# Attention weights transposed by TensorE instead of by DMA, in rounds of three steps placed inside the gemm pieces

## The chip, the cores and the metric

The program runs on one core of a Trainium2 chip. The metric is the device time of one execution in microseconds. Before the change the median of three runs is 3235.93 us (3235.06 to 3238.74).

## The reference

One inference step of a decoder layer. A prompt of 2048 tokens and eight sample tokens go through the same weights, all in float32:

- Mixers: `z = rms_norm(x) @ w_in` with 2304 columns, cut into q, k, v of mixer A (8 heads of 64) and of mixer B (8 query heads, 2 key heads). Mixer A attends in three branches, which are banded attentions over every token, every 4th and every 16th (`DIL_GROUPS = ((128, 1), (512, 4), (2048, 16))`), merged per position by their softmax denominators. Mixer B is banded over 128 keys with a sink per head. Each band: scores of 128 queries against one or two blocks of 128 keys, softmax, weights times values.
- Output projection of both mixers, then cross-attention into 256 memory tokens (its keys and values are `rms_norm(mem) @ w_mem_kv`).
- A feed-forward with a causal convolution of width 3: `w_up` (1024 to 5632), gate, `w_down` (2816 to 1024). Final norm.

The outputs are the prompt's and the samples' rows and the updated key and value caches, so large caches are copied as well.

## The kernel before

**Arithmetic.** A float32 operand is split into a rounded half `hi` (ScalarE) and the rest `lo` (VectorE, or GpSimd), and each product is three matmuls: hi·hi, lo·hi, hi·lo. `hi_of` and `lo_of` (L108 to L120) record these operations for every caller, so most of the splits stand at L110 and L120.

**Stage one** computes the input projection, the attention of both mixers, and the memory keys and values. The projection runs over four groups of 512 tokens and nine blocks of 256 columns, 144 tiles of 128 tokens by 256 columns; `ORDER` names the sequence of groups and columns. `gemm_tile` is one such tile, 24 matmuls of 256 columns (8 depths, three matmuls each; L672 to L674) into one of two PSUM banks `a`. `evac_in` applies rotary with four VectorE operations (or scales on ScalarE) and writes q, k, v to scratch in DRAM. When the columns of a group are done, its attention jobs are queued: kinds `d1`, `d4`, `d16` for mixer A's branches and `b` for mixer B, 64 jobs in all.

A job has two halves of four heads, here called half-jobs, 128 in all. 84 of them have two key blocks and 44 have one. `job_load` (L452, L457) reads a job's rows back from DRAM, and `job_prep` transposes its queries and keys on TensorE (`t_split`, `t_copy`, L473 and L482, through the two PSUM banks `t`) and splits them. A half-job then passes three steps:

- `stage_a`: scores into the banks `se` and `so` (L548; one bank each), masked with a running maximum on VectorE (L556, L559), exponential on ScalarE into `sm` (L561).
- `stage_b`: `sm` to a float16 pair `p2` (L569 ScalarE, L570 VectorE), then one DMA transpose of the whole pair into `pT`, issued on SP's queue (L572).
- `stage_c`: 20 matmuls of 64 columns per key block, `pT` times the values in three bfloat16 parts (L585), copied to `ost` (L592) and stored.

`attn_step` runs one step per call, and three calls are a round: `stage_a` of a new half-job with its `job_prep`, `stage_b` of the one before, and `stage_c` of the one whose transpose was issued two rounds earlier (the queue `ready`). `filler(n)` makes n calls behind each projection tile (2, 3 or 4) and 4 behind each of the 16 tiles of the memory gemm (`mem_gemm`, L1618 to L1620, same size). What is left runs after `mem_pieces`, and the PSUM pool of stage one closes (`p1.close()`) before stage two opens its own.

**Stage two** takes the prompt in four chunks of 512 tokens through output projection, cross-attention and feed-forward: `gemm_b` (L862 to L864), 512 columns a matmul, with the samples' attention, the merges and the cache copies as side work.

**Order.** The program text gives each instruction a priority; the scheduler (`schedule_with_timeline_sim=True`) then fixes the order in which every engine issues, and may place a later instruction ahead of one whose inputs it expects late. On the chip each engine keeps that order. This holds before and after the change, on TensorE too.

Of the kernel before, what the change touches and what calls it, by code (L numbers as in the profile page):

```python
# [35 lines left out]
def tile_layer(ctx: ExitStack, tc: tile.TileContext, I, C, O):  # L36
# [32 lines left out]
    mm = nc.tensor.matmul  # L69
    act = nc.scalar.activation  # L70
# [206 lines left out]
    nc.tensor.transpose(pv[:, 0:120], vrow, ident[:120, :120])  # L277
# [6 lines left out]
    def xprep(key, nxt=None):  # L284
# [3 lines left out]
        def norm():  # L288
            ss = sbL.tile([128, 1], F32, tag="ss", name="ss", bufs=3)
            junk = at_start("sm", 2) if key in range(4) else sbL.tile([128, 1024], F32, tag="xr", name="junk")  # L290
            act(out=junk[:rows], in_=x[:rows], func=ACTF.Square, accum_out=ss[:rows])
            r = sbL.tile([128, 1], F32, tag="r", name="r", bufs=18)
            rms_r(r[:rows], ss[:rows], 1.0 / D, 1, rows)
            rows_r[key] = r

        if key == "s":
            norm()
            pt = bank("t", 2)
            for k in range(8):
                nc.tensor.transpose(pt[:, k * NS:(k + 1) * NS], x[:NS, k * 128:(k + 1) * 128], ident[:NS, :NS])  # L300
# [13 lines left out]
        if key in (1, 2, 3):  # L314
            xr = at_start(*(("p2", 2), ("p2", 2), ("pT", 3))[key - 1]).rearrange("p (k t) -> p k t", k=8)
        else:
            xr = sbL.tile([128, 8, 128], F32, tag="xr", name="xr")
        for hf in range(2):
            pt = bank("t", 2)
            for k in range(4):  # L320
                kk = hf * 4 + k
                nc.tensor.transpose(pt[:, k * 128:(k + 1) * 128], x[:, kk * 128:(kk + 1) * 128], ident)
            act(out=xr[:, hf * 4:hf * 4 + 4, :], in_=pt.rearrange("p (k t) -> p k t", k=4), func=ACTF.Copy)
# [145 lines left out]
    def t_split(ins, hi, lo):  # L469
        pt = bank("t", 2)  # L470
        n = len(ins)
        for i, a in enumerate(ins):
            nc.tensor.transpose(pt[:, i * 128:(i + 1) * 128], a, ident)  # L473
# [4 lines left out]
    def t_copy(ins, out, eng="a"):  # L478
        pt = bank("t", 2)
        n = len(ins)  # L480
        for i, a in enumerate(ins):
            nc.tensor.transpose(pt[:, i * 128:(i + 1) * 128], a, ident)  # L482
        hi_of(out, pt[:, 0:n * 128].rearrange("p (k t) -> p k t", k=n), eng)

    def job_prep(job):
        job.full = job.kind == "d16" or (job.kind == "d4" and job.t == 0)
        if job.kind == "b":
            job.qh = sbR.tile([128, 4, 128], F32R, tag="qh", name="qh", bufs=2)
            job.ql = sbR.tile([128, 4, 128], F32R, tag="ql", name="ql", bufs=2)
            t_split([job.q[:, 128 * j:128 * j + 128] for j in range(4)], job.qh, job.ql)  # L490
            rh, rl = ring("b")
            s = job.t % 2
            t_split([job.k], rh[:, s], rl[:, s])
            job.kh, job.kl = rh, rl
        else:
            if job.full:
                job.qh = sbR.tile([128, 4, 128], F32, tag="qh", name="qf", bufs=2)
                job.kh = sbR.tile([128, 2, 4, 128], F32, tag="kh", name="kf", bufs=1)
                t_copy([job.q[:, 128 * j:128 * j + 128] for j in range(4)], job.qh)
                t_copy([job.k[:, 128 * j:128 * j + 128] for j in range(4)], job.kh[:, 1], "v")  # L500
                job.slots, job.vs, job.mo = [1], [job.v3], None
                job.ost = sbR.tile([128, ST], F32, tag="ost", name="ost", bufs=5)
# [3 lines left out]
            t_split([job.q[:, 128 * j:128 * j + 128] for j in range(4)], job.qh, job.ql)  # L506
            if job.kind == "d1":
                rh, rl = ring("d1")
                s = job.t % 2
            else:  # L510
                rh = sbR.tile([128, 2, 4, 128], F32R, tag="kh", name="kh", bufs=1)
                rl = sbR.tile([128, 2, 4, 128], F32R, tag="kl", name="kl", bufs=1)
                s = 1
            t_split([job.k[:, 128 * j:128 * j + 128] for j in range(4)], rh[:, s], rl[:, s])
            job.kh, job.kl = rh, rl
            if job.kind == "d4" and job.t > 0:
                t_split([job.kp[:, 128 * j:128 * j + 128] for j in range(4)], rh[:, 0], rl[:, 0])
                vprev["d4"] = job.vp3

        v3 = job.v3  # L520
        first = job.kind == "d16" or job.t == 0
        if first:
            job.slots, job.vs, job.mo = [s], [v3], None
        else:
            pv3 = vprev[job.kind]
            if s == 1:
                job.slots, job.vs, job.mo = [0, 1], [pv3, v3], 0
            else:
                job.slots, job.vs, job.mo = [0, 1], [v3, pv3], 1
        if job.kind in ("d1", "b"):  # L530
            vprev[job.kind] = v3
        job.ost = sbR.tile([128, ST], F32, tag="ost", name="ost", bufs=5)

    def stage_a(job, i):
# [15 lines left out]
        sm = sbR.tile([128, 4, 256], F32, tag="sm", name="sm", bufs=2)  # L550
# [62 lines left out]
    quads = deque()  # L613
    loaded = deque()
    pipe = {"b": None}
    ready = deque([None] * 2)
# [3 lines left out]
    def attn_busy():  # L620
        return bool(jobs or loaded or quads or pipe["b"] or any(ready))

    def attn_step():
        if not attn_busy():
# [3 lines left out]
        if s == 0:  # L628
            while len(loaded) < 2 and jobs:
                jb = jobs.popleft()  # L630
                job_load(jb)
                loaded.append(jb)
            if len(quads) == 0 and loaded:
                jb = loaded.popleft()
                job_prep(jb)
                quads.extend([(jb, 0), (jb, 1)])
            pipe["a"] = None
            if quads:
                jb, i = quads.popleft()
                pipe["a"] = (jb, i, stage_a(jb, i))  # L640
                if len(quads) == 0 and loaded:
                    jb = loaded.popleft()
                    job_prep(jb)
                    quads.extend([(jb, 0), (jb, 1)])
        elif s == 1:
            nxt = None
            if pipe["b"]:
                jb, i, sm = pipe["b"]
                nxt = (jb, i, *stage_b(jb, i, sm))
            pipe["b"] = pipe["a"]  # L650
            pipe["n"] = nxt
        else:
            ready.append(pipe["n"])
            if len(ready) > 2:
                e = ready.popleft()
                if e:
                    stage_c(*e)
# [37 lines left out]
    def mem_prep(t):  # L695

        if t == 0:
            while any(jb.kind != "b" for jb in [*jobs, *loaded, *(q[0] for q in quads)]):
# [9 lines left out]
        for hf in range(2):  # L708
            pt = bank("t", 2)
            for k in range(4):  # L710
                kk = hf * 4 + k
                nc.tensor.transpose(pt[:, k * 128:(k + 1) * 128], x[:, kk * 128:(kk + 1) * 128], ident)
# [27 lines left out]
    for oi, (g, js) in enumerate(ORDER):  # L740
        for j in js:
# [4 lines left out]
            for t in range(4):  # L746
# [3 lines left out]
                p = gemm_tile(u, *xT[tt])  # L750
# [4 lines left out]
                filler(4 if j in COLS_B else 2 if oi < 3 else 3)  # L755
# [53 lines left out]
    for a in range(3):  # L809
        n = 128 if a < 2 else 96  # L810
        nc.tensor.transpose(pt[:, a * 128:a * 128 + n], srow[:n, a, :], ident[:n, :n])
# [193 lines left out]
    def sample_softmax(S, nsl, nh, scale, sink, fix):  # L1005
# [6 lines left out]
        for i in range(nb):  # L1012
            nc.tensor.transpose(pt[:w, i * 128:(i + 1) * 128], Sf[:, i * w:(i + 1) * w], ident)
# [165 lines left out]
    def xs_begin():  # L1179
        p = [bankA("t"), bankA("t")]  # L1180
        row = panel32("qxrow")
        for k in range(8):
            nc.tensor.transpose(p[k // 4][:NS, (k % 4) * 128:(k % 4) * 128 + 128], qxs[:, k, :], ident)
# [32 lines left out]
    def xs_fin():  # L1216
        turn_in()
        p = bankA("t")
        for k in range(8):
            nc.tensor.transpose(p[:, k * NS:(k + 1) * NS], osab[:, k * 128:(k + 1) * 128], ident[:NS, :NS])  # L1220
# [20 lines left out]
    def heads_T(c, oT):  # L1241
# [3 lines left out]
        def one(k):  # L1245
            def go():
                pt = bankA("t")
                for i in range(4):
                    nc.tensor.transpose(pt[:, i * 128:(i + 1) * 128],
# [4 lines left out]
                if s_in:  # L1254
                    ps_ = bankA("t")
                    nc.tensor.transpose(ps_[:, 0:NS], osab[:, k * 128:(k + 1) * 128], ident[:NS, :NS])
# [9 lines left out]
    def pre(c, oT, begin):  # L1266
# [108 lines left out]
        def transp(h):  # L1375
            pe = p_t.pop(h)
            pn = [panel("pT"), panel("pT")]
            for kt in range(2):
                pt = bankA("t")
                for t in range(4):  # L1380
                    nc.tensor.transpose(pt[:, t * 128:(t + 1) * 128], pe[t // 2][:, t % 2, kt * 128:kt * 128 + 128], ident)
# [172 lines left out]
    def fin_steps(c, fin):  # L1554
# [4 lines left out]
        def turn(i, hf, pt):  # L1559
            a, n = fin.nt[i]  # L1560
            for k in range(4):
                nc.tensor.transpose(pt[:n, k * 128:(k + 1) * 128], xres[c, 4 * hf + k][:, a:a + n], ident)
# [50 lines left out]
    def mem_gemm(u, h, l):  # L1613
        p = bankA("t")
        for kt in range(8):
            wh, wl = u[kt // 4]
            q = kt % 4
            mm(p[:, 0:256], h[:, kt, :], wh[:, q, :], start=(kt == 0), stop=False)  # L1618
# [4 lines left out]
    def evac_mem(j, t, p, r):  # L1623
# [5 lines left out]
        if j < 4:  # L1629
            dma(out=p_mk[tok, cols], in_=z)  # L1630
            pt = bankA("t")
            for dt in range(2):
                nc.tensor.transpose(pt[:, dt * 128:dt * 128 + 128], z[:, dt * 128:dt * 128 + 128], ident)
# [6 lines left out]
    def mem_pieces():  # L1640
        for j in range(8):
            u = (W.get(), W.get())
            W.ahead(1)
            for t in range(2):
                evac_mem(j, t, mem_gemm(u, *MEM[t][:2]), MEM[t][2])
                filler(4)
# [22 lines left out]
    def conv_out(i):  # L1669
        def go():  # L1670
            gst = small("gst")[:110, 0:128]
            pt = bankA("t")
            nc.tensor.transpose(pt[:110, 0:128], gsave.rearrange("p j f -> p (j f)")[:, i * 110:(i + 1) * 110], ident)
# [83 lines left out]
```

## Time and profile before

| what | value |
|---|---|
| median of 3 runs | 3235.93 us |
| the profiled execution's own time | 3230.24 us |
| its span | 3228.5 us |
| TensorE busy, share of the span | 3100.5 us, 96% |
| VectorE busy | 2147.1 us, 67% |
| ScalarE busy | 1417.1 us, 44% |
| GpSimd busy | 1013.7 us, 31% |
| mean granted clock of TensorE | 0.984 |

The span runs from the first to the last instruction; 1.7 us of the execution's time lie around it. Matmuls are pipelined and the profile models their ends, so the busy share of TensorE says little of how full it is; the distance from one start to the next says more. Stage two begins with the first matmul of L862, at 999 us.

### The profile page before, as it was taken

Reading aid. Unit: us, or ns where it says so; the run is one execution under the profiler, and the core shown is the slowest. Engines: PE = TensorE matmul, PEld = TensorE weight load, DVE = VectorE, ACT = ScalarE, POOL = GpSimd, SP = SyncE. Lnnn points to the kernel's source line nnn. Section 1 sums busy time; section 2 is a strip of 40 time slices with the busy share of each in tenths; the row PEclk is TensorE's granted clock in tenths of the full one; section 3 lists DMA queues with packets and bytes.
Section 4 is the critical chain, followed back from the end, with each engine's and each line's share of the span. In section 5 each row is a group of like instructions: output and inputs, shape, how many; then the busy total and the mean of one; then the engine's idle time right before and its main releaser. Section 6 shows DMA issues by size and latency. Waiting matters only on the chain.

```text
span 3228.5 us, 58044 instructions
## 1 busy us (share of the span) xinstructions
PE 3100.5 (96%) x22290; PEld 2713.9 (84%) x22290; DVE 2147.1 (67%) x4299; ACT 1417.1 (44%) x2793; POOL 1013.7 (31%) x959
## 2 busy tenths in 40 slices
PE   8999989889888999999999999999999999999999
PEld 8998888788877888888887778798877778999998
DVE  7687677787886667665567766555687665554544
ACT  3555654666665444223444333444433343432322
POOL 2711613224244046342205524320554332110102
PEclk9999999998899999999999999999999999999999
DMA  6899999999897346664525555453476445223231
GB/s 211 249 253 237 270 243 230 252 242 220 191 231 230 119 152 209 204 198 162 207 97 184 169 168 183 144 196 111 159 240 235 157 151 179 73 86 96 89 95 64
DMA packets 621837, 580.14 MB, mean 180 GB/s; under 512 B 264140, under 2 KB 554104, under 8 KB 620432
## 3 DMA queue, kind: packets, MB, share of 16 engines
q1 hardware_dynamic: 616808, 572.21, 60.6%
q10 hardware_dynamic: 4608, 4.20, 0.4%
q8 instruction: 175, 2.87, 0.4%
q14 instruction: 102, 0.84, 0.1%
q0 software_dynamic: 144, 0.03, 0.0%
HBM read 457.55 MB, written 136.66 MB: 184 GB/s over the span
## 4 chain that ended last, share of the span: by engine, by line
PE 64%; DVE 7%; DMA 7%; POOL 3%; issue 3%; ACT 2%; SPq 1%; POOLq 0%; DVEq 0%; ACTq 0%
PE g L863 18%; PE g L862 18%; PE g L864 18%; DMA pT<-p 4%; PE s L1358 1%; PE g L1398 1%; PE o L585 1%; DVE wl L120 1%; DVE p L570 1%; DVE sm L556 1%; DMA kx<-in_cache_mem_k_dram 1%; PE g L672 1%; PE g L674 1%; PE g L673 1%; DMA mrg<-o_d 1%
## 5 line engine op out<-in xcount | busy, mean ns | idle before, releaser
L120 DVE TENSOR_TENSOR wl<-wr,wh 128x1024 fp32r<-128x1024 f32 (+1 forms) x406 | 535.7, 1320 | 359.8 <-ACT wh L110 358.3
L110 ACT ACTIVATE wh<-wr 128x1024 fp32r<-128x1024 f32 (+1 forms) x444 | 460.8, 1040 | 674.5 <-PE g L864 382.7
L863 PE MATMUL g<-h,wl 128*128 128x512 f32 (+2 forms) x2080 | 729.5, 351 | 0.0
L862 PE MATMUL g<-h,wh 128*128 128x512 f32 (+2 forms) x2080 | 729.5, 351 | 0.0
L864 PE MATMUL g<-h,wh 128*128 128x512 f32 (+2 forms) x2080 | 725.1, 349 | 0.0
L862 PEld LDWEIGHTS g<-h,wh 128*128 128x128 f32 x2080 | 390.7, 188 | 58.6 <-issue 1.0
L864 PEld LDWEIGHTS g<-h,wh 128*128 128x128 f32 x2080 | 391.2, 188 | 55.2 <-issue 0.5
L863 PEld LDWEIGHTS g<-h,wl 128*128 128x128 f32 x2080 | 390.8, 188 | 54.9 <-issue 1.4
L672 PE MATMUL g<-wh,xh 128*128 128x256 f32 x1152 | 340.4, 296 | 1.1 <-ACT z L383 0.7
L674 PE MATMUL g<-wh,xl 128*128 128x256 f32 x1152 | 333.1, 289 | 0.3 <-DVE xl L120 0.3
L673 PE MATMUL g<-wl,xh 128*128 128x256 f32 x1152 | 331.8, 288 | 0.0
L862 PE MATMUL g<-act,wh 128*128 128x512 f32 (+2 forms) x880 | 310.4, 353 | 8.2 <-ACT act L110 5.7
L863 PE MATMUL g<-act,wl 128*128 128x512 f32 (+2 forms) x880 | 309.4, 352 | 0.0
L864 PE MATMUL g<-act,wh 128*128 128x512 f32 (+2 forms) x880 | 308.0, 351 | 0.0
L561 ACT ACTIVATE sm<-sm,ost 128x256 f32<-128x256 f32 (+1 forms) x512 | 234.8, 460 | 155.1 <-DVE ost L559 154.4
L892 POOL TENSOR_TENSOR sq<-sq 128x512 f32<-128x512 f32 (+1 forms) x83 | 125.2, 1508 | 484.2 <-ACT sq L887 451.3
L672 PEld LDWEIGHTS g<-wh,xh 128*128 128x128 f32 x1152 | 223.5, 194 | 6.4 <-ACT z L383 0.9
L674 PEld LDWEIGHTS g<-wh,xl 128*128 128x128 f32 x1152 | 222.9, 193 | 4.0 <-DVE xl L120 1.2
L673 PEld LDWEIGHTS g<-wl,xh 128*128 128x128 f32 x1152 | 223.3, 194 | 2.1 <-issue 0.2
L862 PE MATMUL g<-oT,wh 128*128 128x512 f32 (+2 forms) x608 | 216.1, 356 | 4.5 <-ACT oT L110 4.5
L863 PE MATMUL g<-oT,wl 128*128 128x512 f32 (+2 forms) x608 | 215.9, 356 | 0.0
L864 PE MATMUL g<-oT,wh 128*128 128x512 f32 (+2 forms) x608 | 211.6, 355 | 0.0
(353 smaller groups left out, 6084.2 us busy)
## 6 DMA issues: line engine op xcount, KB each, us to landing
wr<-in_w_up_dram SPq DMA_DIRECT2D x176, 512.0 KB
wr<-in_w_down_dram SPq DMA_DIRECT2D x80, 512.0 KB
out_dram<-in_cache_a_k_dram SPq DMA_DIRECT2D x32, 1023.5 KB
out_dram<-in_cache_a_v_dram SPq DMA_DIRECT2D x32, 1023.5 KB
wr<-in_w_in_dram SPq DMA_DIRECT2D x60, 512.0 KB
v<-va_d SPq DMA_DIRECT2D x60, 384.0 KB
wr<-in_w_out_dram SPq DMA_DIRECT2D x32, 512.0 KB
wr<-in_w_xq_dram SPq DMA_DIRECT2D x32, 512.0 KB
```

The source lines that it names most:

```text
L110: act(out=out, in_=in_, func=ACTF.Copy)
L120: e.tensor_tensor(out=out, in0=in_, in1=hi.bitcast(F32), op=ALU.subtract)
L556: vec.tensor_tensor_reduce(out=sm[:, x, 0:n], in0=S[e][:, u * n:(u + 1) * n], in1=m_, scale=1.0, scalar=-3e38, op0=ALU.add, op1=ALU.max, a ...
L561: act(out=sm[:, x, 0:n], in_=sm[:, x, 0:n], func=ACTF.Exp, scale=0.125, bias=nb[:, x:x + 1], accum_out=job.ost[:, 520 + 4 * i + x:521 + 4 ...
L570: vec.tensor_tensor(out=p2[:, 1], in0=sm[:, :, 0:n], in1=p2[:, 0], op=ALU.subtract)
L672: mm(p[:, 0:256], h[:, kt, :], wh[:, q, :], start=(kt == 0), stop=False)
L673: mm(p[:, 0:256], h[:, kt, :], wl[:, q, :], start=False, stop=False)
L674: mm(p[:, 0:256], l[:, kt, :], wh[:, q, :], start=False, stop=(kt == 7))
L862: mm(o, wh[:, q, c], pn[:, 0, a:b], start=st, stop=False)
L863: mm(o, wl[:, q, c], pn[:, 0, a:b], start=False, stop=False)
L864: mm(o, wh[:, q, c], pn[:, 1, a:b], start=False, stop=en)
L892: pl.tensor_tensor(out=acc[:, 0:self.ncol], in0=acc[:, 0:self.ncol], in1=sq[:, 0:self.ncol], op=ALU.add)
```

## The change

The float16 pair and the DMA transposes are gone. `stage_b` now transposes the weights `sm` themselves on TensorE, four blocks of 128x128 for each key block, into a bank `t`; ScalarE copies that bank to float16 and VectorE subtracts to get the rest, both into `pT`. There are 212 such banks (84 half-jobs with two, 44 with one), so 848 transposes, 212 copies and 212 subtractions. `sm` has four buffers for two, and `p2` none.

`job_prep` returns its parts (queries, keys, keys before) as steps. A round's steps are now: `stage_a` of a new half-job; `stage_c` of the half-job two rounds back and behind it `stage_b` of the one before; the preparation of the next job. `gemm_tile` makes its calls between the depths of its 8 instead of behind the tile, as many calls as before (`mem_gemm` likewise). `tr` is only a name for `nc.tensor.transpose`.

```diff
     def stage_b(job, i, sm):
 
-        n = 128 * len(job.slots)
-        p2 = sbR.tile([128, 2, 4, n], F16, tag="p2", name="p2", bufs=2)
-        act(out=p2[:, 0], in_=sm[:, :, 0:n], func=ACTF.Copy)
-        vec.tensor_tensor(out=p2[:, 1], in0=sm[:, :, 0:n], in1=p2[:, 0], op=ALU.subtract)
-        pT = sbR.tile([128, 16, 128], F16, tag="pT", name="pT", bufs=3)[:, 0:n // 16]
-        nc.sync.dma_start_transpose(out=pT, in_=p2.rearrange("p g x k -> p (g x k)"))
-        v = pT.rearrange("p (g x h) t -> p g h x t", g=2, x=4)
-        return v[:, 0], v[:, 1]
+        nh = len(job.slots)
+        pT = sbR.tile([128, 2, 2, 4, 128], F16, tag="pT", name="pT", bufs=3)
+        for hf in range(nh):
+            pt = bank("t", 2)
+            for x in range(4):
+                tr(pt[:, x * 128:(x + 1) * 128], sm[:, x, hf * 128:(hf + 1) * 128], ident)
+            v = pt.rearrange("p (x t) -> p x t", x=4)
+            act(out=pT[:, 0, hf], in_=v, func=ACTF.Copy)
+            vec.tensor_tensor(out=pT[:, 1, hf], in0=v, in1=pT[:, 0, hf], op=ALU.subtract)
+        return pT[:, 0], pT[:, 1]
...
     def attn_step():
...
         if s == 0:
-            while len(loaded) < 2 and jobs:
...
+            fetch()
+            if cur[0] is None:
+                begin_prep()
+                while to_prep:
+                    to_prep.popleft()()
+                cur[:] = [nxt[0], 0]
+                nxt[0] = None
+            pipe["n"] = None
+            if cur[0]:
+                jb, i = cur
+                pipe["n"] = (jb, i, stage_a(jb, i))
+                cur[:] = [jb, 1] if i == 0 else [None, 0]
         elif s == 1:
-            nxt = None
             if pipe["b"]:
-                jb, i, sm = pipe["b"]
-                nxt = (jb, i, *stage_b(jb, i, sm))
-            pipe["b"] = pipe["a"]
-            pipe["n"] = nxt
+                stage_c(*pipe["b"])
+            pipe["b"] = None
+            if pipe["a"]:
+                jb, i, sm = pipe["a"]
+                pipe["b"] = (jb, i, *stage_b(jb, i, sm))
+            pipe["a"] = pipe["n"]
         else:
-            ready.append(pipe["n"])
-            if len(ready) > 2:
-                e = ready.popleft()
-                if e:
-                    stage_c(*e)
+            begin_prep()
...
-    def gemm_tile(u, h, l):
+    def gemm_tile(u, h, l, steps=0):
         p = bankA("g")
         for kt in range(8):
             wh, wl = u[kt // 4]
             q = kt % 4
+            if kt * steps // 8 > (kt - 1) * steps // 8 and kt:
+                filler(1)
...
-                p = gemm_tile(u, *xT[tt])
+                p = gemm_tile(u, *xT[tt], 4 if j in COLS_B else 2 if oi < 3 else 3)
...
-                filler(4 if j in COLS_B else 2 if oi < 3 else 3)
+                filler(1)
```

How the instructions stand in the two built programs shows at three places. The first is SP's queue in the middle of stage one, before the change; `raw` and `v` are a job's rows, `wr` a weight tile, `ka_d` and `va_d` the scratch of keys and values, `o_d` the attention's output, `pT` the transposed weights.

```order
L572 DMA_TRANSPOSE pT<-p_6374 128x16x128
L608 DMA o_d_70<-ost 128x528
L385 DMA va_d<-vs 128x768
L452 DMA raw<-ka_d 128x512
L141 DMA wr_6807<-in_w_in_dram 128x4x256
L452 DMA raw<-qa_d 128x512
L572 DMA_TRANSPOSE pT<-p_6508 128x16x128
L457 DMA v_6347<-va_d 128x1536
```

After the change SP's queue holds the same kinds of rows without any transpose (128 before, none now).

The second place is TensorE in the same part of the program, after the change: `g` is a projection tile's bank, `sm` the weights, `t` a transpose's bank, `se` and `so` the score banks.

```order
L694 MATMUL g<-wh_3116,xl 128x256
L548 MATMUL se<-kh,qh 128x256
L548 MATMUL so<-kh,qh 128x256
...
L572 MATMUL t<-ident,sm 128x128 x4
L692 MATMUL g<-wh_3116,xh 128x256
L693 MATMUL g<-wl_3117,xh 128x256
L548 MATMUL se<-kl,qh 128x256
...
L572 MATMUL t<-ident,sm 128x128 x4
L694 MATMUL g<-wh_3116,xl 128x256
```

The transposes of one half-job now stand between the scores of the next and pieces of a projection tile; before, nothing of `stage_b` stood on this engine.

The third place is TensorE at the end of stage one, behind the memory gemm (`mh`, bank `t`). Before the change (`mg` are merged outputs, `oT` the first operand of stage two, `v3b` mixer B's values):

```order
L1620 MATMUL t<-wh_16776,mh 128x256
L585 LDWEIGHTS pT
L585 MATMUL o<-v3b,pT 128x64
...
L1249 MATMUL t<-ident,mg 128x128 x6
...
L1249 MATMUL t<-ident,mg 128x128 x2
L862 MATMUL g<-oT,wh_16782 128x512
```

After it:

```order
L1642 MATMUL t<-wh_17799,mh 128x256
L1269 MATMUL t<-ident,mg 128x128 x4
L548 MATMUL se<-ringb_13522,qh 128x256 x2
...
L474 MATMUL t<-ident,raw 128x128 x4
...
L572 MATMUL t<-ident,sm 128x128 x4
...
L587 MATMUL o<-v3b,pT 128x64
```

Behind the memory gemm the weight·value matmuls (L585, now L587) of 2 half-jobs were left, and now of 11; behind the last projection tile those of 21 (840 of 4240 matmuls), and now of 41 (1640). The scheduler has moved projection tiles ahead of attention.

## Rows read from the trace of the kernel before

**Rows 1.** The page's slices: the span in 40 parts, shares in tenths

```profile
PE   8999989889888999999999999999999999999999
...
PEclk9999999998899999999999999999999999999999
DMA  6899999999897346664525555453476445223231
```

**Rows 2.** Windows: us, each engine's busy time, granted clock, DMA share, GB/s

```profile
0.00:125.00 125.00, 111.61 (x892) 106.55 (x893) 86.39 (x175) 47.81 (x83) 55.59 (x62) 1.00 0.71 219
125.00:859.00 734.00, 669.95 (x7900) 620.50 (x7898) 570.09 (x1794) 439.51 (x1224) 223.45 (x219) 0.95 0.99 239
859.00:999.00 140.00, 111.89 (x1505) 100.93 (x1503) 116.01 (x329) 92.04 (x250) 65.84 (x44) 0.95 1.01 240
999.00:3228.50 2229.50, 2207.05 (x11998) 1885.89 (x11998) 1374.59 (x2004) 837.77 (x1239) 668.82 (x635) 0.99 0.46 154
```

**Rows 3.** The page's chain of waits, shares of the span by line

```profile
PE g L863 18%; PE g L862 18%; PE g L864 18%; DMA pT<-p 4%; PE s L1358 1%; PE g L1398 1%; PE o L585 1%; DVE wl L120 1%; DVE p L570 1%; DVE sm L556 1%; DMA kx<-in_cache_mem_k_dram 1%; PE g L672 1%; PE g L674 1%; PE g L673 1%; DMA mrg<-o_d 1%
```

**Rows 4.** Tile `pT`, 125 to 859 us: its issues, who waited (us, times)

```profile
L572 SPq DMA_TRANSPOSE pT<-p x109: 1231/2430/7324, 128.4 to 857.8; - x109
...
  DMA pT<-p: 70.2, 54
```

**Rows 5.** The same tile, 859 to 999 us

```profile
  DMA pT<-p: 26.6, 20
```

**Rows 6.** Timeline of TensorE where it waits for `pT` (brackets: idle before)

```profile
764.47 1.03 PE L585 MATMUL o<-v,pT 128*128 128x64 bf16 x16 [1.68 <-DMA pT<-p]
...
770.56 0.41 PE L674 MATMUL g<-wh,xl 128*128 128x256 f32 x1
770.77 0.41 PE L672 MATMUL g<-wh,xh 128*128 128x256 f32 x1
```

**Rows 7.** Windows around that wait, columns as in rows 2

```profile
760.00:765.00 5.00, 3.32 (x52) 2.69 (x49) 4.88 (x9) 1.90 (x4) 4.98 (x5) 0.51 0.72 154
765.00:770.00 5.00, 5.00 (x47) 4.37 (x44) 3.77 (x20) 3.13 (x9) 1.89 (x5) 0.50 0.90 202
```

**Rows 8.** Timeline of TensorE at 441 us: start us, us, what

```profile
441.79 0.38 PE L548 MATMUL se<-kh,qh 64*128 64x256 f32 x1
...
442.71 1.09 PE L473 MATMUL t<-ident,raw 128*128 128x128 f32 x8
443.63 1.33 PE L585 MATMUL o<-v,pT 128*128 128x64 bf16 x40
444.80 0.37 PE L672 MATMUL g<-wh,xh 128*128 128x256 f32 x1
...
448.78 0.28 PE L672 MATMUL g<-wh,xh 128*128 128x256 f32 x1
```

**Rows 9.** Groups by line, whole span: busy us, mean ns, idle before

```profile
L570 DVE TENSOR_TENSOR p<-sm,p 128x1024 f16<-128x1024 f32 (+1 forms) x128 | 156.7, 1224 | 58.0 <-ACT p L569 57.5
L569 ACT ACTIVATE p<-sm 128x1024 f16<-128x1024 f32 (+1 forms) x128 | 115.9, 905 | 55.5 <-DMA pT<-p 54.1
```

**Rows 10.** Groups by line and shape, whole span: bank `t` to a pair

```profile
L120 DVE TENSOR_TENSOR ql<-t,qh 128x512 fp32r<-128x512 f32 x44 | 29.9, 680 | 2.1 <-ACT qh L110 2.1
L110 ACT ACTIVATE qh<-t 128x512 fp32r<-128x512 f32 x44 | 25.8, 587 | 20.5 <-PE t L473 14.2 <-DMA pT<-p 3.8 <-PE so L548 2.5
```

**Rows 11.** Groups by line and shape, TensorE, 125 to 859 us

```profile
L473 PE MATMUL t<-ident,raw 128*128 128x128 f32 x296 | 45.3, 286 | 3.1 <-DVE ql L120 1.7 <-DMA raw<-ka_d 1.4
```

**Rows 12.** Timeline of SP's queue, a transpose and what follows it

```profile
871.84 4.24 SPq L572 DMA_TRANSPOSE pT<-p  x1
876.12 1.05 SPq L948 DMA_DIRECT2D mg<-o_d  x2
```

**Rows 13.** Windows, columns as in rows 2

```profile
300.00:600.00 300.00, 267.22 (x3111) 248.49 (x3111) 209.17 (x643) 166.88 (x462) 108.21 (x118) 0.95 1.02 250
```

**Rows 14.** The page's DMA packets by size

```profile
DMA packets 621837, 580.14 MB, mean 180 GB/s; under 512 B 264140, under 2 KB 554104, under 8 KB 620432
```

More of the change, by code (lines that the diff above doesn't have):

```diff
@@ L69, in tile_layer @@
     mm = nc.tensor.matmul
+    tr = nc.tensor.transpose
     act = nc.scalar.activation
@@ L276, in tile_layer @@
     pv = bankA("pv")
-    nc.tensor.transpose(pv[:, 0:120], vrow, ident[:120, :120])
+    tr(pv[:, 0:120], vrow, ident[:120, :120])
     vec.tensor_copy(out=vecs, in_=pv[:, 0:120])
@@ L289, in norm @@
             ss = sbL.tile([128, 1], F32, tag="ss", name="ss", bufs=3)
-            junk = at_start("sm", 2) if key in range(4) else sbL.tile([128, 1024], F32, tag="xr", name="junk")
+            junk = at_start("sm", 4) if key in range(4) else sbL.tile([128, 1024], F32, tag="xr", name="junk")
             act(out=junk[:rows], in_=x[:rows], func=ACTF.Square, accum_out=ss[:rows])
@@ L486, in job_prep, with queries @@
         job.full = job.kind == "d16" or (job.kind == "d4" and job.t == 0)
[L487 to L495, printed above, removed]
+        cols = [slice(128 * j, 128 * j + 128) for j in range(4)]
+        def queries():
             if job.full:
                 job.qh = sbR.tile([128, 4, 128], F32, tag="qh", name="qf", bufs=2)
[L498 to L502, printed above, removed]
+                t_copy([job.q[:, c] for c in cols], job.qh)
                 return
@@ L515, in job_prep @@
[L515 to L529, printed above, removed]
@@ L534, in stage_a, with before @@
+        def before():
+            t_split([job.kp[:, c] for c in cols], job.kh[:, 0], job.kl[:, 0])
+        return [queries, keys] + ([before] if job.kind == "d4" and job.t > 0 else [])
     def stage_a(job, i):
@@ L620, in attn_busy, with attn_left, fetch, begin_prep @@
     def attn_busy():
-        return bool(jobs or loaded or quads or pipe["b"] or any(ready))
+        return bool(jobs or loaded or to_prep or nxt[0] or cur[0] or pipe["a"] or pipe["b"])
+    def attn_left():
+        return [*jobs, *loaded] + [j for j in (nxt[0], cur[0]) if j]
+    def fetch():
+        while len(loaded) < 2 and jobs:
+            jb = jobs.popleft()
+            job_load(jb)
+            loaded.append(jb)
+    def begin_prep():
+        if nxt[0] is None and loaded:
+            nxt[0] = loaded.popleft()
+            to_prep.extend(job_prep(nxt[0]))
     def attn_step():
@@ L628, in attn_step @@
         if s == 0:
[L629 to L644 removed]
+            fetch()
[10 more added lines that the diff above has]
+                cur[:] = [jb, 1] if i == 0 else [None, 0]
         elif s == 1:
[L646 removed]
             if pipe["b"]:
[L648 to L657 removed]
+                stage_c(*pipe["b"])
[4 more added lines that the diff above has]
+            pipe["a"] = pipe["n"]
+        else:
+            begin_prep()
+            if cur[0] is not None:
+                if len(to_prep) > 1 and nxt[0] is not None and not hasattr(nxt[0], "qh"):
+                    to_prep.popleft()()
+            else:
+                while to_prep:
+                    to_prep.popleft()()
         return True
@@ L697, in mem_prep @@
         if t == 0:
-            while any(jb.kind != "b" for jb in [*jobs, *loaded, *(q[0] for q in quads)]):
+            while any(jb.kind != "b" for jb in attn_left()):
                 filler(1)
```

83 lines of the change are left out of this document (51 added, 32 removed).

## The prediction, blind

> **What bounds the kernel now.** I read the slices first, to see which engine is full where: TensorE is at 8 or 9 tenths throughout, its clock dips in slices 10 and 11, and the DMA engines are at 8 or 9 tenths up to slice 12 and far below behind it [rows 1]. The windows cut this at four milestones: the first 24 projection tiles (0 to 125 us), the tiles with attention between them (125 to 859, called B), what is left behind the last projection tile (859 to 999, called C), and stage two [rows 2]. In stage two TensorE is busy 2207 of 2229.5 us; nothing the change touches stands there, so the whole effect must come from B and C, 874 us. There TensorE is busy 670 of 734 and 112 of 140 us, at a granted clock of 0.95, and the DMA engines' share is 0.99 and 1.01.
>
> The chain of waits then tells what stands late: behind the matmuls of stage two the DMA into `pT` is the largest single item, 4% of the span [rows 3]. The view of that tile gives the size: in B engines sat idle 70.2 us in 54 waits for the transposes' DMA [rows 4], in C 26.6 us [rows 5]. A wait costs more than itself. At 764.47 us a group of weight·value matmuls starts after 1.68 us of idle time, and six microseconds later two gemm matmuls still start 0.21 us apart [rows 6]; the granted clock in those ten microseconds is 0.51 and 0.50, which is the 1.2 GHz level [rows 7].
>
> How full is TensorE in B really? At the 2.4 GHz level 33 gemm matmuls start within 444.80 to 448.78 us, 0.12 us each; eight fp32 transposes take 443.63 − 442.71 = 0.92 us, 0.115 each; 40 weight·value matmuls take 1.17 us; twelve score matmuls (as six pairs) 0.92 us [rows 8]. A projection tile is then 24 × 0.12 = 2.9 us. A mean half-job has 4240/128 = 33 weight·value matmuls (0.97 us); its scores I put at 0.73 and its share of the preparation's transposes at 0.46, together 2.16 us. B holds 120 tiles and some 85 half-jobs: 348 + 184, and 20 for the rest, 552 us of work. Of the 182 us of B that are not work, 70 are the waits for `pT`, 0.05 × 734 = 37 are the clock, and 75 are other waits.
>
> **The change part by part.** *TensorE gains 848 transposes*, four a bank for 212 banks: 848 × 0.115 = 97.5 us [rows 8], 0.76 us a half-job, which makes 2.92. All of this is on the engine that is nearly full. But the order of the built program also moves half-jobs: 41 instead of 21 stand behind the last projection tile, so B keeps about 65 of 85. Its work becomes 348 + 65 × 2.92 + 20 = 558 us, 6 more than before, and the added transposes' price is paid in C.
>
> *The waits for `pT` go*: −70 in B. What is late next is the hand-over through a bank: the values' matmuls need ScalarE's copy and VectorE's subtraction of a 128x512 bank, 0.587 and 0.680 us by the same operations of the preparation [rows 10]. Such a step lies between pieces of a gemm tile, so it should be hidden; if its cover is gone it costs at most 1.27 us a bank, for 65 × 212/128 = 108 banks of B 137 us, and at least nothing. The nearest row is the preparation's own transposes into the same banks: 3.1 us of idle time for 296/8 = 37 groups, 0.08 us each [rows 11]. I take it: +9.
>
> *The clock*: B's 37 us can shrink to nothing or stay. Since a wait of 1.68 us cost ten microseconds at half speed [rows 7], I hold the 54 waits for most of it and take −30.
>
> *Fewer half-jobs in B*: the 75 us of other waits go with the attention; 20 of 85 fewer give −18 (none to −75).
>
> *VectorE and ScalarE*: VectorE loses L570, 156.7 us, and gains 212 × 0.680 = 144.2; ScalarE loses L569, 115.9, and gains 212 × 0.587 = 124.4 [rows 9, 10]. −12 and +9 us over all of stage one, both engines under 80% busy in B, no term of the sum there. The finer steps add no instruction.
>
> *SP's queue*: 128 transposes go. One holds the queue 4.24 us before the next transfer issues [rows 12]; the median in B is 2.43 us [rows 4]. The loads of rows and weights that stood behind them come earlier. I give it no term beyond the waits already counted, and the first rival its chance.
>
> *C*: 20 more half-jobs without projection tiles between them. TensorE alone would need 2.92 us for each. C as it is takes 140/21 = 6.7 us for each half-job with all else in it. VectorE, the fullest engine there, is busy 116.0 us, 5.5 for each of the 21 [rows 2], of which some belongs to the memory tiles and merges, which don't grow. I take 5.0, with 2.9 and 6.7 as ends: C = 140 + 20 × 5 = 240 us (198 to 274). The 26.6 us of `pT` waits in C I don't take off, since VectorE at 83% is right behind them.
>
> Sum: B = 734 + 6 − 70 + 9 − 30 − 18 = 631. Stage one = 125 + 631 + 240 = 996 us instead of 999: −3. The profiled execution took 3230.24 us (span 3228.5 and 1.7 around it), 5.7 below the median of the runs; taken from the median, 3236 − 3 = 3233 us. So the forecast is no change: the transposes that leave the DMA come back on TensorE and in a longer uncovered end. Its own range is 3207 to 3257: C may miss by 42 below and 34 above, the clock's term by 7 and 30, the bank's by 9 and more, and I let about half of these fall together.
>
> **The rivals.** *First, faster: the DMA side was the limiter of B.* Between 300 and 600 us the DMA share is 1.02, VectorE is busy only 209 of 300 us and TensorE is not full either [rows 13]. The transposes make up most of the packets under 512 bytes, 264140 of 621837 [rows 14], and hold SP's queue some 128 × 2.43 = 311 us [rows 4]. If row and weight loads late behind them cause the 75 us of other waits too, B loses another 30 and C starts with its rows loaded, 220: stage one 945, 3182 us. Against it: the idle time put down to other DMAs is small, 1.4 us at the preparation [rows 11]. It would show as B near 600 us.
>
> *Second, slower: the two banks `t` become the wait.* TensorE keeps its issue order, and 212 new groups of transposes share two banks with the preparation. If each waits half of the 1.27 us until copy and subtraction have freed a bank, 108 × 0.64 = 69 us in place of the 9: stage one 1056, 3293 us. It decides from about 0.17 us a bank on (9 + 3 + 6.5 over 108). For it: ScalarE and VectorE take work in order too, so a 0.68 us subtraction stands behind other VectorE rows; against it the 0.08 us of today [rows 11].
>
> *Third, slower: the clock doesn't recover.* With a transpose group and small matmuls between gemm pieces the granted clock may fall by another 0.05 in B and C: 0.05 × (631 + 240) = 44 us, 3277 us. Against it, the eight transposes at 442.71 us and what follows them run at full pace [rows 8]. The Trainium skill, page "TensorE: Matmul & The Clock Gate", section "Part 4: PE-mode transpose", says that transposes don't count as busy time for the clock in the way matmuls do; the spacing of [rows 8] doesn't show it, but that is eight transposes inside dense work.
>
> *Fourth: the change doesn't do what it says.* By the built order a part of the half-jobs gets no gemm pieces around it at all; that is in the forecast already, as C.
>
> **How the numbers follow.** Forecast 0.46, first rival 0.27, second 0.20, third 0.07. Within 0.2% (6.5 us, about what a measurement of this kernel can tell from no change) lies a part of the forecast alone: 0.15. Of its rest 0.18 are faster, 0.13 slower. Faster: 0.27 + 0.18 = 0.45; slower: 0.20 + 0.07 + 0.13 = 0.40. The range for 8 in 10 reaches past the first rival's and the second's times: 3170 to 3300; the likeliest case alone has 3207 to 3257.
>
> **What would show it.** In the profile after: first matmul of L882 near 996 us; last projection tile near 756 (125 + 631); no wait for `pT`'s DMA, and less than 0.1 us of idle time for each new group of transposes; clock 0.98 or more in B; DMA share in B near 0.7; VectorE the fullest engine from 756 us on, with about 5 us a half-job. Wrong would be: B under 610 us (first rival), idle time at the transposes or the values' matmuls put down to ScalarE and VectorE of 20 us or more in B (second), a clock of 0.90 (third), or a stage two that is not 2229 us.

## The result, and the profile after

The changed kernel took 3328.72 us (median of four runs, 3318.16 to 3330.28) against 3235.49 us: a ratio of 1.0284, 95% interval 1.0257 to 1.0311. It is 93 us slower; the forecast was 3233 us, and the time lies outside its range of 3170 to 3300.

The profiled execution took 3318.16 us, its span is 3316.4. It is the fastest of the four (the others took 3328 to 3330 us) and 88 us longer than the profiled one before, so the trace has 88 of the 93 us to explain. First the page's slices (rows as in [rows 1]) and its packets [rows 14]:

```profile
PE   8999999999888999999999999999999999999999
...
PEclk9999999999799999999999999999999999999999
DMA  7765655665152534656453545453466445222322
...
DMA packets 400659, 524.65 MB, mean 158 GB/s; under 512 B 42957, under 2 KB 332921, under 8 KB 399249
```

There are 221178 packets fewer, and the clock's dip has moved from slices 10 and 11 to one at slice 11. The windows show where the time went. The last projection tile is at 791.1 us now, stage two begins at 1087.7 (columns as in [rows 2]):

```profile
125.00:791.10 666.10, 650.08 (x7263) 607.01 (x7263) 481.61 (x1542) 364.28 (x1034) 189.79 (x212) 0.99 0.62 183
791.10:1087.70 296.60, 247.43 (x2985) 215.47 (x2984) 204.28 (x663) 177.01 (x525) 67.90 (x51) 0.89 0.36 112
1087.70:3316.40 2228.70, 2205.36 (x12005) 1883.75 (x12001) 1374.22 (x2004) 838.58 (x1237) 668.39 (x636) 1.00 0.46 154
```

Stage two is as long as before, 2228.7 against 2229.5 us. B went from 734 to 666 us and C from 140 to 297, with 41 half-jobs instead of 21 behind the last tile. In C no engine is full: TensorE is busy 83%, VectorE 69%, ScalarE 60% of the time, and the granted clock is 0.89. What TensorE's matmuls wait for from 104 us to stage two is in the view of waits (engine, bank, line <- releaser: us, times, longest). First the largest row before the change, then the largest rows after it:

```profile
PE o L585 <- DMA pT<-p: 43.1, 34, 2.8
```

```profile
PE o L587 <- ACT pT L574: 22.4, 20, 2.3
PE t L474 <- DVE pT L575: 11.5, 17, 2.7
PE o L587 <- DVE pT L575: 6.0, 10, 1.4
PE se L548 <- DVE mx L556: 5.5, 4, 2.8
```

Nothing waits for `pT`'s DMA any more; 40 us of waits for ScalarE's copy (L574) and VectorE's subtraction (L575) of the new banks stand where 43 us stood, 35 of them in C. The timeline in C shows one such wait grow (start us, us, engine, line):

```profile
866.49 0.51 ACT L561 ACTIVATE sm<-sm,ost 128x256 f32<-128x256 f32 x1 [1.52 <-DVE ost L559]
...
867.15 1.92 PE L572 MATMUL t<-ident,sm 128*128 128x128 f32 x8 [0.67 <-ACT sm L561]
...
869.96 0.50 ACT L561 ACTIVATE sm<-sm,ost 128x256 f32<-128x256 f32 x1
...
870.55 1.06 ACT L574 ACTIVATE pT<-t 128x512 f16<-128x512 f32 x2
...
871.17 0.69 DVE L575 TENSOR_TENSOR pT<-t,pT 128x512 f16<-128x512 f32 x1
...
871.19 0.34 PE L587 MATMUL o<-v3b,pT 128*128 128x64 bf16 x3 [2.12 <-ACT pT L574]
...
871.84 0.69 DVE L575 TENSOR_TENSOR pT<-t,pT 128x512 f16<-128x512 f32 x1
871.91 0.47 PE L474 MATMUL t<-ident,rawb 128*128 128x128 f32 x1 [0.39 <-DVE pT L575]
```

Eight transposes fill both banks from 867.15 us on, behind four exponentials of their half-job (L561, the first at 866.49), and are through after 1.92 us. ScalarE has four more exponentials ahead of its copies, those of another half-job (the last at 869.96), and the copies start at 870.55. The values' matmuls, next on TensorE, wait 2.12 us for the first copy; three matmuls later TensorE needs a bank for the next job's keys, both are still held, and it waits again until VectorE has subtracted. The first bank is held 4.7 us (867.15 to 871.86, the end of the first subtraction) for a copy and a subtraction of 1.3 us together.

### The profile page after: what moved, and what is told of

Its sections match the earlier page's. It is cut to its first block, busy times and chain, and to the rows that moved or that the text cites. A ratio compares the mean times of both kernels' runs of the same rounds, so it can differ in the third digit from the quotient of the medians.

```text
span 3316.4 us, 59587 instructions
## 1 busy us (share of the span) xinstructions
PE 3214.5 (97%) x23138; PEld 2812.3 (85%) x23138; DVE 2146.7 (65%) x4383; ACT 1428.1 (43%) x2877; POOL 980.2 (30%) x959
## 4 chain that ended last, share of the span: by engine, by line
PE 76%; DVE 8%; DMA 5%; POOL 4%; ACT 3%; issue 3%; SPq 0%; POOLq 0%; ACTq 0%; DVEq 0%
PE g L883 17%; PE g L882 17%; PE g L884 17%; PE g L692 3%; PE g L694 3%; PE g L693 3%; PE o L587 3%; PE se L548 2%; PE t L572 2%; ACT sm L561 2%; PE s L1378 1%; DMA mrg<-o_d 1%; PE g L1418 1%; DVE wl L121 1%; POOL mrg L1010 1%
## 5 line engine op out<-in xcount | busy, mean ns | idle before, releaser
L561 ACT ACTIVATE sm<-sm,ost 128x256 f32<-128x256 f32 (+1 forms) x512 | 236.0, 464 | 102.3 <-DVE ost L559 93.9
L882 PE MATMUL g<-oT,wh 128*128 128x512 f32 (+2 forms) x608 | 215.4, 355 | 1.6 <-ACT oT L111 1.6
L587 PEld LDWEIGHTS <-pT 128*128 128x128 f16 x4240 | 166.3, 102 | 59.0 <-ACT pT L574 27.9
```

Of the source, the lines that this page charges most:

```text
L561: act(out=sm[:, x, 0:n], in_=sm[:, x, 0:n], func=ACTF.Exp, scale=0.125, bias=nb[:, x:x + 1], accum_out=job.ost[:, 520 + 4 * i + x:521 + 4 ...
L587: mm(o, p_[:, hf, x, :], v[:, g, :], start=(x == 0 and hf == 0 and n_ == 0), stop=(hf == nh - 1 and n_ == 4), skip_group_check=True)
L882: mm(o, wh[:, q, c], pn[:, 0, a:b], start=st, stop=False)
```

## The experiments

The runs come in five groups, the kernel before beside each (3235 to 3238 us). "Left" is the number of half-jobs whose values stand behind the last projection tile; it is 21 before and 41 in the changed kernel. "Gaps" is the time in which TensorE started nothing, from 104 us to stage two, worked out from the traces: of each start-to-start distance of two matmuls over 0.6 us, what exceeds 0.125 us (about a gemm matmul's own). Gaps are 99 us before and 67 in the changed kernel; the rest of that stretch, called work, is 796 and 916. So TensorE's work grew by 120 us and its gaps shrank by only 32, which is the 88 us. "Half clock" is the time of that stretch in which the granted clock is at the 1.2 GHz level: 82 us before, 14 of them in C, and 75 in the changed kernel, 65 of them in C. As an estimate it costs half of itself, and nearly all of that stands in the work.

**One part at a time.** *pe_old_steps*: the kernel before with the new `stage_b` alone (and its four buffers `sm`).

```diff
-        act(out=p2[:, 0], in_=sm[:, :, 0:n], func=ACTF.Copy)
...
-        nc.sync.dma_start_transpose(out=pT, in_=p2.rearrange("p g x k -> p (g x k)"))
...
+            for x in range(4):
+                nc.tensor.transpose(pt[:, x * 128:(x + 1) * 128], sm[:, x, hf * 128:(hf + 1) * 128], ident)
+            v = pt.rearrange("p (x t) -> p x t", x=4)
+            act(out=pT[:, 0, hf], in_=v, func=ACTF.Copy)
+            vec.tensor_tensor(out=pT[:, 1, hf], in0=v, in1=pT[:, 0, hf], op=ALU.subtract)
```

> The kernel before, with only stage_b replaced: transposes on TensorE, copy and subtraction from PSUM; steps, fillers behind the tiles and the queue 'ready' as before. 1040 weight-value matmuls (26 half-jobs) stand behind the last tile. Price of the transposes: 106 us of TensorE less some 50 of waits, 3280 to 3310 us. Order: with 26 instead of 41 half-jobs uncovered 3230 to 3260 us.

3265.9 us (1.0095, 1.0079 to 1.0110), 31 us slower than before, between the two theories' ranges: the work is 892 us, 96 more than before, and the gaps are 32, 67 less. *dma_new_steps*: the other half, the new steps and placement with the DMA transposes. It keeps the queue `ready`, which the changed kernel lacks.

```diff
+        nc.sync.dma_start_transpose(out=pT, in_=p2.rearrange("p g x k -> p (g x k)"))
...
-            if pipe["b"]:
-                stage_c(*pipe["b"])
+            ready.append(pipe["b"])
+            e = ready.popleft()
+            if e:
+                stage_c(*e)
```

> The changed kernel's steps and placement inside the gemm tiles, with the float16 pair and the DMA transposes of before (values two rounds behind the transpose). 24 half-jobs stand behind the last tile. Price of the transposes: 3215 to 3245 us, the placement is worth little either way. Order: placement itself is the harm, 3260 us or more.

3239.5 us (1.0016, 1.0006 to 1.0027): +4. The parts cost 31 and 4, both together 93: 58 us lie in what they do to each other, the missing queue included. Against pe_old_steps the changed kernel has 35 us more gaps and 24 us more work; its half clock is 75 us against 27, which by the estimate is those 24.

*twice*: every transpose of the weights issued two times.

```diff
-            for x in range(4):
+            for x in (0, 1, 2, 3, 0, 1, 2, 3):
```

> The changed kernel with every transpose of the weights issued twice into the same place (848 more on TensorE, nothing else). Price of the transposes: +95 to +125 us over the changed kernel, 3420 to 3455 us. If they lay in TensorE's idle time instead: +20 us or less.

3383.7 us, +55 over the changed kernel: neither theory's number. 848 more transposes cost 0.065 us each where they take 0.11 (58 us for 524 in B). The rest comes back elsewhere: the gaps fell from 67 to 55 us and the half clock from 75 to 31. In B the granted clock is 0.99 with twice as many transposes.

**The order.** *text_order*: each matmul and transpose of stage one tied behind the one recorded before it.

```diff
-    mm = nc.tensor.matmul
-    tr = nc.tensor.transpose
+                with tc.issue_after(pe_last[0].ins):
+                    r = op(*a, **k)
...
+    mm = in_order(nc.tensor.matmul)
+    tr = in_order(nc.tensor.transpose)
```

> The changed kernel with TensorE held to the order of the program text in stage one (each of its instructions behind the one before). By the text 760 of the 4240 weight-value matmuls (19 half-jobs) stand behind the last projection tile; the scheduler left 1640 (41). Theory 'price of the transposes' (TensorE was already the bound; 848 transposes cost what they take): little is won, 3300 to 3340 us. Theory 'order' (half-jobs left without gemm pieces cost the 88 us): most of it comes back, 3235 to 3270 us.

3431.8 us, another 103 slower, outside both ranges, with only 19 half-jobs left. So the scheduler's moving of projection tiles was not the harm; it hid a part of it (the edit also undoes every other move on TensorE, and what each of them is worth is not shown). With the order held TensorE waits for the banks in plain sight, 67 of the 86 us ahead of the last tile, where the changed kernel hardly waits (all matmuls have the helper's line here, L76; `t` is the bank, L589 the subtraction):

```profile
PE t L76 <- DVE pT L589: 85.9, 58, 4.2
```

*bounded*: a milder edge; `last_v` is the last matmul that `stage_c` has recorded, `m` its value six tiles before.

```diff
+        if kt == 0 and len(marks) > 6:
+            m = marks.popleft()
+            if m is not None:
+                with tc.issue_after(m):
+                    return mm(*a, **k)
...
+        marks.append(last_v[0])
```

> The changed kernel, in which a projection tile's first matmul must stand behind the last weight-value matmul that the text had recorded six tiles before; all else is left to the scheduler. 28 half-jobs stand behind the last tile instead of 41 (26 where the old steps were kept). Theory 'tail' (a half-job costs about 8 us behind the last tile and 4.3 between tiles): 13 x 3.7 us come back, 3270 to 3295 us. Theory 'steps' (the finer steps inside a tile cost TensorE their waits wherever the half-jobs stand): 3320 to 3350 us.

3319.0 us (1.0260, 1.0241 to 1.0279) with 28 left: 13 half-jobs fewer in C bought 10 us, not 48, and the changed kernel's own executions lie as far apart (3318 to 3330). The gaps only moved: 45 us in B and 26 in C, where the changed kernel has 16 and 50. The theory of the tail falls.

**The banks.** *three_t* and *old_steps_three_t*: one edit on the changed kernel and on pe_old_steps. The third bank `t` is taken from `o`, the values' output, which keeps one.

```diff
-        pt = bank("t", 2)
+        pt = bank("t", 3)
-        po = bank("o", 2)
+        po = bank("o", 1)
```

> The changed kernel with three banks t and one bank o in stage one. 35 half-jobs stand behind the last tile. Theory 'banks' (two banks t shared by preparation and weights make TensorE wait): 3250 to 3290 us, with the idle time put down to L575 gone. Theory 'tail' alone: 6 half-jobs x 3.7 us, 3300 to 3315 us. If the single bank o hurts more: above 3328 us.

> The old steps with all transposes on TensorE (3266 us), with three banks t and one o. 21 half-jobs stand behind the last tile instead of 26. Theory 'banks': 3225 to 3250 us. Theory 'tail' alone: 5 x 3.7 us, about 3248 us. If the single bank o hurts: 3266 us or more.

3256.2 us (1.0058, 1.0038 to 1.0077), 72 less than the changed kernel; and 3212.65 us (0.9926, 0.9912 to 0.9940), 53 less than with two banks, more than either theory had, and faster than the kernel before. In three_t the two waits that stood first are almost gone, and C's clock is back (waits; then windows, 125 us to the last tile and on to stage two):

```profile
PE se L548 <- DVE mx L556: 8.0, 8, 2.1
PE o L587 <- DVE pT L575: 5.6, 15, 0.8
PE o L587 <- ACT pT L574: 3.5, 5, 1.9
```

```profile
125.00:809.20 684.20, 673.22 (x7671) 629.49 (x7670) 511.81 (x1622) 384.00 (x1101) 195.15 (x211) 0.99 0.62 184
809.20:1028.20 219.00, 197.55 (x2588) 175.34 (x2584) 180.39 (x583) 151.45 (x456) 65.73 (x51) 0.96 0.42 132
```

Gaps fell from 67 to 31 us, the work from 916 to 893 and the half clock from 75 to 34. On the old steps the gain is of another kind: gaps fell by 5 us only (32 to 27), the work by 44. *before_three_t*, the control, is the same edit on the kernel before.

> The kernel before with three banks t and one o, all transposes by DMA: the control for the banks. Theory 'banks of the new transposes': its preparation alone uses the banks, so 3225 to 3240 us. If the bank helps whatever uses it: 3190 to 3215 us, and then the transposes on TensorE win nothing.

3230.9 us (0.9979, 0.9967 to 0.9991): −7 us. The third bank is worth much only where the weights' transposes use it. *half_half* and *half_three_t* let the second half-job of each job transpose on TensorE and the first by DMA, with two and with three banks (and three buffers `sm`).

```diff
+        if i == 1:
...
+                    nc.tensor.transpose(pt[:, x * 128:(x + 1) * 128], sm[:, x, hf * 128:(hf + 1) * 128], ident)
...
+            return pT[:, 0], pT[:, 1]
-        p2 = sbR.tile([128, 2, 4, n], F16, tag="p2", name="p2", bufs=2)
+        p2 = sbR.tile([128, 2, 4, n], F16, tag="p2", name="p2", bufs=1)
```

> The kernel before, in which only the second half-job of each job transposes on TensorE (424 transposes) and the first by DMA. If the waits for the DMA's transposes come from its throughput, half of them removes nearly all 97 us of waits for half the price on TensorE (about 50 us): 3190 to 3225 us. If they are plain latency, half of the waits and half of the price: 3235 to 3255 us.

> Second half-jobs' transposes on TensorE, first ones' by DMA (3236 us), with three banks t and one o. Theory 'banks': 424 transposes gain about half of what 848 gained (53 us): 3205 to 3220 us. If the bank helps little here: 3230 us or more.

3236.3 us (1.0003, 0.9992 to 1.0013) and 3212.05 us (0.9921, 0.9903 to 0.9939): the third bank gives 24 us to 424 transposes and 53 to 848. half_three_t and old_steps_three_t beat both kernels, and cannot be told apart.

**A false trail.** In old_steps_three_t all score matmuls take 122 us of TensorE, in pe_old_steps 151 (distances to the next start, each counted up to 0.6 us); the scheduler had left fewer runs of one bank (152 against 365 followed by one of the same). *before_paired*, *after_paired*, *old_steps_paired* and *three_t_paired* hold the scores in the text's order.

```diff
-                    mm(S[e][:, u * n:(u + 1) * n], q_[r, p, :], k_[r, s0:s0 + nh, pk, :],
+                    with tc.issue_after(last) if last else nullcontext():
+                        last = mm(S[e][:, u * n:(u + 1) * n], q_[r, p, :], k_[r, s0:s0 + nh, pk, :],
...
```

> The kernel before, in which each half-job's score matmuls keep the order of the text (se and so in turn). In the trace of before 918 score matmuls are followed by one of the other bank and take 65 us, 285 by one of the same bank and take 43; all scores 150 us. Theory 'pairs' (two matmuls on different 64 rows run beside each other, so the scheduler's runs of one bank cost TensorE time): scores 120 to 125 us, and 3205 to 3225 us. If TensorE's waits take it back: 3230 to 3245 us.

> The changed kernel with the same edge on the scores (359 followed by one of the same bank before, 0 now). Theory 'pairs': 25 to 35 us less than the changed kernel, 3293 to 3303 us. Theory 'banks' (its loss is two banks t): the half-jobs wait as before, 3315 to 3335 us.

> The old steps with all transposes on TensorE and two banks t (3266 us), with the same edge on the scores. With three banks t it was 3213 us, and its scores fell from 151 to 122 us of TensorE. Theory 'pairs': the third bank only changed the scheduler's order, 3230 to 3245 us here. Theory 'banks': 3255 us or more.

> The new steps with three banks t and one o (3256 us), with the same edge on the scores. If the rest of its distance to the old steps with three banks (44 us) is the order of the scores (149 against 122 us of TensorE): 3220 to 3235 us. If it is the steps themselves: 3250 us or more.

3239.5, 3317.6, 3267.9 and 3254.7 us: +3, −11, +2 and −1, the −11 again within what the changed kernel's executions differ by. In before_paired 65 scores are followed by one of the same bank instead of 285, and all scores still take 146 us instead of 150; 206 instead of 173 are now followed by other work, and those got longer. The theory of the pairs falls. Why the scores take less in old_steps_three_t stays open, and they are 29 of the 44 us of work that the third bank saved there.

**What is left of the steps.** *after_later* and *three_t_later* put the queue `ready` back between the transposes and the values (the diff's lines as in dma_new_steps, with TensorE's transposes).

> The changed kernel with the values' matmuls one round later behind the weights' transposes (a queue between the two, as the kernel before had). Theory 'distance' (TensorE waits 43 us where it reaches the values before copy and subtraction are done): 3270 to 3295 us, and under 10 us of those waits. Theory 'pieces' (calls between a tile's depths cost it, wherever the values stand): 3315 to 3335 us.

> The same with three banks t and one o (3256 us without the later values). Theory 'distance': 3212 to 3235 us, as the old steps with three banks (3213 us). Theory 'pieces': 3245 us or more.

3308.2 us (1.0216, 1.0195 to 1.0237) and 3240.7 us (1.0009, 0.9996 to 1.0022): 20 us with two banks, 15 with three, each between its theories' ranges. The waits for copy and subtraction at the values fell less than expected with two banks (17.7 us for the copy are left); with three, TensorE's waits are small. The two edits together return 88 of the 93 us; gaps are 25 us then, the work 870, the half clock 3. Then the placement alone: *old_three_t_inside* is old_steps_three_t with this edit, *three_t_later_behind* three_t_later with its reverse (the memory gemm likewise).

```diff
-                filler(4 if j in COLS_B else 2 if oi < 3 else 3)
+                filler(1)
+            if kt * steps // 8 > (kt - 1) * steps // 8 and kt:
+                filler(1)
```

> The old steps, transposes on TensorE, three banks t (3213 us), with the calls between the depths of a gemm tile as in the changed kernel. Theory 'pieces' (the placement costs the 28 us that are left): 3235 to 3250 us. Theory 'round' (what a round's steps hold, preparation split off, costs them): 3205 to 3222 us.

> The new steps with three banks t and later values (3241 us), with all calls behind the tile as in the kernel before. Theory 'pieces': 3208 to 3222 us. Theory 'round': 3233 to 3250 us.

3213.9 us (3212.65 with the calls behind the tile) and 3239.3 (3240.7 inside). With three banks it makes no difference where the calls stand. The last 28 us between new and old steps lie in what a round holds (preparation split off, values and transposes in one step); which of these it is stays open. Between the traces of three_t_later and old_steps_three_t 20 us show, and 19 of them are the scores' distances (141 and 122 us).

## Why the prediction was wrong

**The step that failed is the hand-over of a bank: "I take it: +9" for B, and no term for it in C.** Two edits, a third bank and a round between transposes and values, return 88 us: by the traces 42 us of gaps and 46 of work, of which the half clock, 75 us against 3, makes some 36 by the estimate. I took the price of 0.08 us from the preparation's own transposes [rows 11], which had the two banks to themselves, and bounded it by 1.27 us, copy plus subtraction [rows 10]. Both are too low for the same reason: a bank is held from the first transpose until the subtraction ends, and other work can stand first on the engines that empty it. In the timeline above the bank is held 4.7 us, with four exponentials ahead of the copy on ScalarE and VectorE waiting for that copy. The rival "the two banks `t` become the wait" had the mechanism and nearly the size (stage one 1056 us forecast, 1088 measured), with 0.20 to the forecast's 0.46. Its place was off. In B, where the 9 stood, such waits are 6 us, and all gaps 16, since the scheduler put projection tiles into the waits; these ran out 68 us sooner, and in C, where the half-jobs were left, little covered a bank's wait. So the loss was given back later, and text_order shows it where it arises.

**C: 240 forecast, 297 measured.** 20 more half-jobs cost 7.8 us each, above my upper end of 6.7. I took VectorE for the bound there; at 69% it wasn't. In three_t, which leaves 35 half-jobs, C is 219 us: 5.6 for each of the 14 more than before, near my 5.0. So what I lacked in C is the wait for the banks, and the clock that fell with it.

**B: 631 forecast, 666 measured.** Two readings behind the sum were wrong. The first is "−70": the 70.2 us of [rows 4] are two rows of one wait, TensorE's weight loads and the matmuls behind them (tile `pT` before, 125 to 859 us, who waited):

```profile
  PEld L585: 39.1, 29
  PE o L585: 31.1, 25
```

Each of the 25 waits lies in one of the 29, so TensorE had 31 to 39 us to win there, not 70. The second is "some 85 half-jobs": 3400 weight·value matmuls over the 40 of a half-job with two key blocks. B held 107 (by the copies of L592), and 33 matmuls and 2.16 us are the mean over all. The change adds 87 × 2.92 − 107 × 2.16 = 23 us of work and not 6. With both put right the same sum gives B = 734 + 23 − 31 + 9 − 30 − 18 = 687 and stage one 1052, 53 us more than before and not 3 less. B itself took 21 less than that.

"552 us of work" was too low as well: by the distances, B before was 666 us of work and 68 of gaps. The 22 half-jobs make 48 of the 114 us that were missing. Most of the others come from prices that I took from the best stretch [rows 8]: over B a gemm matmul takes 0.131 us, and the scores 118 us in all, where 107 × 0.73 are 78. An engine with 9% of gaps, not 25%, has no room for 97 us of transposes.

The clock rose to 0.99 in B, as written, and by the estimate gave back about the 30 us (68 us of half clock in B before, 10 after). But the wait of [rows 6] didn't cost the ten microseconds of [rows 7]: it begins at 762.8 us, and the clock record has the 1.2 GHz level from 760.1 on.

**The other rivals.** The DMA as B's limiter: its share fell from 0.99 to 0.62 and B didn't come down to 600 us; half_half, with half of that traffic and 424 transposes in its place, takes the time of before. The clock: it is 0.99 in B with 524 transposes between the matmuls and, in twice, with 1077, so the transposes themselves don't lower it there; the 0.89 of C goes with the waits, and is 0.96 in three_t with the same transposes. The Trainium skill, page "TensorE: Matmul & The Clock Gate", section "Part 4: PE-mode transpose", says that the full clock "doesn't engage" for transposes; among matmuls, as here, the trace gives that no price, and no run here has transposes alone. That the new steps cost nothing by themselves held with DMA transposes (+4 us) and not with TensorE's.

**The three-bank version with later values shows the time without these waits:** its stage two begins at 999.6 us, where I had 996 for the changed kernel (windows of three_t_later, to the last tile and on to stage two):

```profile
125.00:846.30 721.30, 704.48 (x8326) 658.91 (x8325) 547.06 (x1784) 419.82 (x1223) 196.47 (x213) 1.00 0.60 181
846.30:999.60 153.30, 145.85 (x1936) 132.94 (x1934) 125.31 (x422) 114.17 (x337) 59.84 (x47) 1.00 0.51 160
```

The forecast left the banks' waits out, but that its total fits here is luck: the parts are 721 and 153 us with 25 half-jobs left, not 631 and 240 with 41; the sum held two misreadings; and this execution is the fastest of ten, 9 us below their median.

## What to carry to other kernels

When work moves from a DMA to an engine, price the buffer that it passes through, not only the instructions: how long each buffer is held is set by what stands in the queues of the engines that empty it, and the number of buffers decides whether the next producer waits. An engine's free time is the sum of its gaps between starts over the whole stretch, not the stretch less a count priced at the best spacing. A list of who waited for a tile can hold one wait twice, as TensorE's weight load and as its matmul; take the row of the matmuls. And a scheduler that moves independent work into waits hides the loss at first; look at what is left when that work has run out.

## What the runs showed of the hardware

The 128 DMA transposes made 221178 of the 621837 packets; in pe_old_steps, where `stage_b` alone is new, the DMA share up to the last tile is 0.60 against 0.99. fp32 transposes of 128x128 among other matmuls start 0.110 us apart in B at a granted clock of 0.99; in C they start 0.15 us apart, at 0.89 and in part behind exponentials, as in the timeline above.
